# Four seven-product units and one plain unit in the feed-forward stage, in place of three and three

## The chip, the cores and the metric

The kernel runs on one core of a Trainium2 chip. The metric is the device time of one execution in microseconds (us). Five engines take part: PE (TensorE, matmuls; PEld is its weight load), DVE (VectorE), ACT (ScalarE), POOL (GpSimd) and SP (SyncE, which here only issues DMAs). Each engine works through its own instructions in a fixed order and waits for the others by semaphores.

## The reference

One decoder layer in float32 on x of 256 positions by 1024 columns. The first half (block-sparse and differential attention, gates, output projection) is not touched by the change. The second half is

```
x = x + RMSNorm_post(SwiGLU(RMSNorm_pre(x)))
SwiGLU(h) = (silu(h @ w_gate) * (h @ w_up)) @ w_down
# w_gate, w_up: 1024 x 2816    w_down: 2816 x 1024
```

The result has to be accurate to float32. The kernel writes a float32 number as a high part (rounded to PE's fp32r) and a low part (the remainder) and takes three matmuls for one product: high x high, low x high, high x low.

## The kernel before, in words

**f's and units.** The 2816 columns of gate and up are 22 blocks f of 128. The first four are done in another form; the list UNITS (line 54) gives the others: R at f = 4, W at 6, R at 10, W at 12, R at 16, W at 18. The 256 positions are two blocks t = 0 and t = 1 of 128.

**A plain unit (R, line 1140 on)** computes gate and up of two f's: 4 weight pieces, 48 matmuls of 512 columns.

**A seven-product unit (W, line 1090 on)** computes gate and up of four f's, for both t, as a 2 x 2 block product with seven products in place of eight, called 11, T1, T2, 22, T3, 21 and T4. Each has two weight pieces (a and b, 128 x 1024 "pages") and 12 matmuls of 512 columns. The pages of T1 and T3 are sums of two weights: POOL issues DMAs that add the second onto the first (L176). T2 = 11 + T3 and T4 = T2 + 21 are added on DVE (L282), two pages each; in the last unit T4 is made by accumulating DMAs (L288). The products are combined by DVE operations of 128 x 512: u0, u1, the add and the multiply of g0 (around a Silu on ACT) and the multiply of g1 (behind another Silu). The result for t = 0 is called s (or s2), that for t = 1 is called g (or g1).

**Splits.** Each weight piece is split by ACT (copy to the high part, L195) and DVE (subtract for the low part, L198). High and low parts lie in a ring of WB = 5 pairs: the split of a piece can only begin when PE has finished with the piece five places before it. Pages that were loaded lie in 12 buffers, which SP refills (L173) when DVE and ACT have let go of them.

**Down projection.** For each f, PE transposes s and g, ACT takes the high part of the transposed block and DVE the low part (the tile fT), and a weight piece of w_down (wraw) is split; 12 matmuls of 512 columns, called z here, add the result into banks acc. The transposes of a unit's four f's come in the unit behind it, in two sets: first t = 0 (s), then t = 1 (g), both into the same bank, which exists once. So the second set waits until ACT and DVE have read the first. The first set stands behind product 11 and the second behind T1. For t = 1, the second half of the columns goes into two banks of 256 columns each (acc and pv).

**Order.** The order of PE is the list of slots; plan_W gives the places of the products and of z in a unit: 11, T1, T2, z, 22, z, T3, 21, z, T4 in the middle. The order of ACT, DVE and POOL is written out while the slots are walked: granules_ahead (line 404) lets the splits run four pieces ahead of PE, and the operations of a unit that follow a product are put behind the slot that ends it.

**End.** The last four f's of w_down (18 to 21) are split early into memory of their own (wextra) at places given by TAIL_AT, and are used when all else is done: first t = 0, then t = 1, whose second half is done in two pieces of 256, so that the norm of the first piece (ACT L923, DVE L927) can run beside the matmuls of the second.

Of the kernel before, what the change touches and what calls it, by code (L numbers as in the profile page):

```python
# [35 lines left out]
NFF = DFF // P  # L36
# [14 lines left out]
RB = 7  # L51
NWARM = 13
NAT = 4
UNITS = [("R", 4), ("W", 6), ("R", 10), ("W", 12), ("R", 16), ("W", 18)]


def _slopes():
# [8 lines left out]
def tile_hybrid_block(  # L66
# [201 lines left out]

    NTAIL = 4

    TAIL_AT = {"T2": (NFF - 4,), "22": (NFF - 3,), "21": (NFF - 2,), "T3": (NFF - 1,)}
    dr = [raw1(w_down, f * P, 1, 0, 1024) for f in range(NFF)]
    for f in range(NFF):
        dr[f]["name"] = ("d", f)
# [65 lines left out]

    for ui, (kind, f0) in enumerate(UNITS):
        if kind == "R":
            rr = [raw_of([(slice(0, 256), rows(w_gate, 2 * kc * P, 2, f0 * P, 256)),
                          (slice(256, 512), rows(w_up, 2 * kc * P, 2, f0 * P, 256))], 2) for kc in range(4)]
            todo = [lambda kc=kc: job_split(("r", f0, kc), rr[kc]) for kc in range(4)]
            if ui == 0:
                uns = [lambda kc=kc: job_split(("un", kc), nr["un", kc]) for kc in range(1, 4)]
                todo = uns[0:1] + s_jobs(0) + uns[1:2] + s_jobs(1) + uns[2:3] + s_jobs(2, 3, 4, 5) + todo[0:2] + \
                    s_jobs(6) + todo[2:3] + s_jobs(7, 8) + todo[3:4]
            ds = [lambda i=i: job_split(("d", i), dr[i]) for i in units_before(ui)]  # L350
            if ui == 0:
                first = raws_of_W(UNITS[1][1])
                add1 = [lambda i=i: job_add(first["T1"][i], first["11"][i], first["12"][i]) for i in range(2)]
                ds[2:3] += add1[0:1]
                ds += add1[1:2]
            todo += ds
        else:
            b, todo = raws_of_W(f0) if ui > 1 else first, []
            for n in ("11", "T1", "T3", "22", "21"):
                for r in b[n]:  # L360
                    touch(r)
            for n in plan_W(ui):
                if n[0] == "z":
                    todo.append(lambda f=n[1]: job_split(("d", f), dr[f]))
                    continue
                for i in range(2):
                    if n == "T1":
                        todo.append(lambda i=i: job_split(("T1", f0, i), b["T1"][i]))
                        todo.append(lambda i=i: job_add(b["T2"][i], b["11"][i], b["T3"][i]))
                    else:  # L370
                        todo.append(lambda n=n, i=i: job_split((n, f0, i), b[n][i]))
                    if n == "11" and ui == 1:
                        todo.append(lambda i=i: job_add(b["T3"][i], b["12"][i], b["22"][i]))
                    if n == "T2" and ui == len(UNITS) - 1:
                        todo.append(lambda i=i: job_more(b["T2"][i]))
                    if i == 1 and ui == len(UNITS) - 1:
                        for f in TAIL_AT.get(n, ()):
                            todo.append(lambda f=f: job_split(("d", f), dr[f]))
                    if n == "21" and ui < len(UNITS) - 1:
                        todo.append(lambda i=i: job_add(b["T4"][i], b["T2"][i], b["21"][i]))  # L380
        for f in todo:
            f()
# [21 lines left out]
    def granules_ahead(slots, n, most, late):  # L404

        def f(i):
            j, seen = i + 1, set()
            while j < len(slots) and j - i <= most:
                seen |= {x for x, _ in slots[j]["need"]} - {x for x, _ in slots[i]["need"]}
                if len(seen) > n - (i >= len(slots) - late):  # L410
                    break
                j += 1
            return j - i - 1
        return f
# [443 lines left out]
    def out_part(z, name, lhs, ks, t, hf, last, pieces=None):  # L858
        for k in ks:
            for c0, c1, bank in pieces or z[t]:  # L860
                if c0 // 512 == hf:
                    mm3(bank[:, 0:c1 - c0], lhs(k, t), [v[:, 0, c0:c1] for v in W((name, k))],
                        start=k == 0, stop=k == last)

    zb = []

    def z_slots(name, k, lhs, last):
        def pe(hf):
            if not zb:
                zb.extend([(0, 512, ps("acc")), (512, 1024, ps("acc"))] for _ in range(NT))  # L870
                if name == "d":
                    zb[1][1:] = [(512, 768, zb[1][1][2]), (768, 1024, ps("pv"))]
            for t in range(NT):
                out_part(zb, name, lhs, [k], t, hf, last)
        return [dict(pe=lambda h=h: pe(h), need=[((name, k), h)]) for h in range(2)]

    def z_tail(name, ks, lhs, t, last):

        if name == "d" and t == 1:
            return [dict(pe=lambda i=i: out_part(zb, name, lhs, ks[2 * i:2 * i + 2], t, 0, last),  # L880
                         need=[((name, k), 0) for k in ks[2 * i:2 * i + 2]]) for i in range(2)] + \
                   [dict(pe=lambda i=i: out_part(zb, name, lhs, ks, t, 1, last, [zb[t][1 + i]]),
                         need=[((name, k), 1) for k in ks]) for i in range(2)]
        return [dict(pe=lambda h=h, i=i: out_part(zb, name, lhs, ks[2 * i:2 * i + 2], t, h, last),
                     need=[((name, k), h) for k in ks[2 * i:2 * i + 2]]) for h in range(2) for i in range(2)]
# [4 lines left out]
    zgs = []  # L890
# [17 lines left out]
    slots = []  # L908
# [184 lines left out]
    def unit_W(ui, f0, ring):  # L1093

        st, made = {}, {}
        banks = dict(zip("acb", ring))

        def bank(n):
            if n not in st:
                st[n] = ps(banks[n])  # L1100
            return st[n]

        def slots_of(n, bk, a, start, post):
            return [dict(pe=lambda kp=kp: block(bank(bk), a, n, f0, kp, start, True), need=[((n, f0, kp), 0)],
                         post=[lambda: active.append(post())] if kp else []) for kp in range(2)]

        def copy(n, tag, bk, **kw):
            def f():
                made[n] = work.tile([P, 512], F32, tag=tag, name=n, **kw)
                nc.scalar.activation(made[n], st[bk], AF.Copy)  # L1110
                yield
            return f

        def u1():
            nc.vector.tensor_tensor(made["v5"], made["v5"], st["a"], op=OP.subtract)
            yield

        def u0():
            u = made["s2"]
            nc.vector.tensor_tensor(u, st["c"], u, op=OP.subtract)  # L1120
            yield

        def g0():
            g = made["s1"]
            nc.vector.tensor_tensor(g, st["b"], g, op=OP.add)
            yield
            nc.scalar.activation(g, g, AF.Silu, scale=rs2[:, 0:1])
            yield
            u = made["s2"]
            nc.vector.tensor_tensor(u, u, g, op=OP.mult)  # L1130

        def g1():
            g = made["g1"] = work.tile([P, 512], F32, tag="e", name="g1", bufs=4)
            nc.scalar.activation(g, st["a"], AF.Silu, scale=rs2[:, 1:2])
            yield
            nc.vector.tensor_tensor(g, g, made["v5"], op=OP.mult)

        how = {"11": ("a", A(0, 0), True, copy("s1", "ph0", "a", bufs=1)),
               "T1": ("c", R_(0), True, copy("v5", "pl0", "c", bufs=1)),
               "T2": ("a", R_(1), False, copy("s2", "e", "a", bufs=4)), "22": ("c", R_(3), False, u0),  # L1140
               "T3": ("a", R_(2), False, u1), "21": ("b", A(0, 1), True, g0), "T4": ("a", A(1, 1), False, g1)}
        sl = [s for n in plan_W(ui) for s in (z_slots("d", n[1], f_of, NFF - 1) if n[0] == "z" else slots_of(n, *how[n]))]
        return sl, [lambda tag: f_T({0: lambda: made["s2"]}, f0, 4, tag), lambda tag: f_T({1: lambda: made["g1"]}, f0, 4, tag)]

# [64 lines left out]


    def norm3(t):
        pn.append(post_norm(zb[t], gp2, eps3[:, t:t + 1], zgs[t]))
        pn[t][0](0)

    def finish(t):
        piece, r, zg = pn[t]
        piece(len(zb[t]) - 1)
        for c0, c1 in ((0, 384), (384, 768), (768, 1024)):
            add_x(zg, zg, r, xt[:, t, :], c0, c1)
            nc.sync.dma_start(out[0, t * P:(t + 1) * P, c0:c1], zg[:, c0:c1])  # L1220
# [33 lines left out]
```

## Time and profile before

| | us |
|---|---|
| median of 3 runs (lowest to highest) | 382.33 (381.61 to 383.94) |
| the profiled execution's own time | 383.71 |
| its span | 381.9 |
| PE busy | 369.8 (97%) |
| DVE busy | 300.2 (79%) |
| ACT busy | 233.9 (61%) |
| POOL busy | 43.8 (11%) |
| mean granted clock of PE | 0.993 |

The span is the time from the first to the last instruction of the profiled execution. Busy times overlap. A start-to-start distance shorter than the duration means that an engine begins the next instruction before the last one's end. In the trace, whi and wlo are the high and low parts in the ring, wpage and wraw the loaded pieces, h2h and h2l the normalized x. The feed-forward units from W6 on lie at 237 to 262 (W6), 262 to 286 (R10), 286 to 311 (W12), 311 to 334.5 (R16) and from 334.5 on (W18).

### The profile page before, as it was taken

The page shows a single profiled execution, that of the slowest core. Times are in us where ns is not written, and L with a number is a line of the kernel's source. Part 1 is how long each engine was busy: PE and PEld are TensorE (multiplying, and loading weights), DVE is VectorE, ACT ScalarE, POOL GpSimd, SP SyncE. Part 2 cuts the span into 40 slices and gives each one's busy share as a digit, 9 for nine tenths or more (in the row PEclk, how much of TensorE's full clock was granted, in tenths as well). Part 3 has the DMA queues.
Part 4 walks back from the last instruction along what each step waited for, and adds up shares of the span by engine and source line. Part 5 has one row for each costly group of instructions (what it writes and reads, how often), then busy time and mean ns, then how long its engine had stood idle before and what let it go on. Part 6 is the DMA issues. An engine that isn't in the chain of part 4 may idle for free.

```text
span 381.9 us, 6158 instructions
## 1 busy us (share of the span) xinstructions
PE 369.8 (97%) x2212; PEld 324.4 (85%) x2212; DVE 300.2 (79%) x542; ACT 233.9 (61%) x431; POOL 43.8 (11%) x61
## 2 busy tenths in 40 slices
PE   6999999999999999999999999999999999999893
PEld 4799989999999999898888888888888888888683
DVE  3799787899978757798669969998578885799534
ACT  3985576768665865574469453866548655487221
POOL 0099600000001000000000000220002200020000
PEclk9999999999999999999999999999999999999898
DMA  6988746253654553587216998899959997151003
GB/s 191 389 288 306 207 128 206 66 167 111 218 156 127 184 198 128 187 250 230 92 57 204 399 391 277 207 329 289 379 166 191 342 298 217 57 83 27 3 0 110
DMA packets 41665, 74.98 MB, mean 196 GB/s; under 512 B 3218, under 2 KB 15523, under 8 KB 41635
## 3 DMA queue, kind: packets, MB, share of 16 engines
q1 hardware_dynamic: 38914, 69.36, 54.3%
q0 software_dynamic: 2720, 5.24, 8.0%
q8 instruction: 17, 0.28, 0.3%
q14 instruction: 14, 0.11, 0.1%
HBM read 73.54 MB, written 1.05 MB: 195 GB/s over the span
## 4 chain that ended last, share of the span: by engine, by line
PE 88%; DVE 5%; DMA 2%; issue 2%; ACT 2%; SPq 1%; POOLq 0%; DVEq 0%; ACTq 0%
PE acc L227 14%; PE acc L228 13%; PE acc L229 13%; PE acc L663 5%; PE sb L227 4%; PE sb L228 4%; PE sb L229 4%; PE sa L228 4%; PE sa L227 4%; PE sa L229 4%; PE t L227 3%; PE t L228 3%; PE t L229 3%; DVE wlo L198 3%; PE pv L228 2%; PE pv L229 2%
## 5 line engine op out<-in xcount | busy, mean ns | idle before, releaser
L198 DVE TENSOR_TENSOR wlo<-wraw,whi 128x512 fp32r<-128x512 f32 (+1 forms) x137 | 116.7, 873 | 35.7 <-ACT whi L195 35.3
L195 ACT ACTIVATE whi<-wraw 128x512 fp32r<-128x512 f32 (+1 forms) x136 | 99.2, 765 | 31.0 <-PE acc L228 14.5
L227 PE MATMUL acc<-hTh,whi 128*128 128x256 f32 x256 | 73.1, 286 | 0.5 <-DVE q L602 0.5
L229 PE MATMUL acc<-hTh,wlo 128*128 128x256 f32 x256 | 71.8, 281 | 0.0
L228 PE MATMUL acc<-hTl,whi 128*128 128x256 f32 x256 | 71.8, 281 | 0.0
L198 DVE TENSOR_TENSOR wlo<-wpage,whi 128x1024 fp32r<-128x1024 f32 x42 | 50.8, 1220 | 8.4 <-ACT whi L195 8.2
L195 ACT ACTIVATE whi<-wpage 128x1024 fp32r<-128x1024 f32 x42 | 43.9, 1060 | 18.7 <-PE pv L229 8.4
L227 PEld LDWEIGHTS acc<-hTh,whi 128*128 128x128 f32 x256 | 48.3, 189 | 0.8 <-DVE q L602 0.7
L228 PEld LDWEIGHTS acc<-hTl,whi 128*128 128x128 f32 x256 | 48.3, 189 | 0.0
L229 PEld LDWEIGHTS acc<-hTh,wlo 128*128 128x128 f32 x256 | 48.2, 188 | 0.0
L227 PE MATMUL acc<-whi,fT 128*128 128x512 f32 x72 | 26.5, 368 | 0.0
L229 PE MATMUL acc<-whi,fT 128*128 128x512 f32 x72 | 26.2, 365 | 0.0
L228 PE MATMUL acc<-wlo,fT 128*128 128x512 f32 x72 | 26.2, 364 | 0.0
L176 POOL DMA_DIRECT2D wpage<-in_w_up_dram x8 | 9.8, 1225 | 89.6 <-DMA wpage<-in_w_gate_dram 70.5
L708 ACT ACTIVATE e<-e,nmx 128x256 f32<-128x256 f32 (+1 forms) x32 | 14.3, 447 | 5.7 <-DVE nmx L705 5.4
L282 DVE TENSOR_TENSOR wpage<-wpage 128x1024 f32<-128x1024 f32 x14 | 17.0, 1217 | 0.0
L228 PEld LDWEIGHTS acc<-wlo,fT 128*128 128x128 f32 x72 | 13.5, 188 | 2.6
L227 PEld LDWEIGHTS acc<-whi,fT 128*128 128x128 f32 x72 | 13.5, 188 | 2.5
L229 PEld LDWEIGHTS acc<-whi,fT 128*128 128x128 f32 x72 | 13.5, 188 | 2.3
L227 PE MATMUL t<-whi,h2h 128*128 128x512 f32 x36 | 15.1, 420 | 0.0
L228 PE MATMUL t<-wlo,h2h 128*128 128x512 f32 x36 | 15.0, 416 | 0.0
L229 PE MATMUL t<-whi,h2l 128*128 128x512 f32 x36 | 14.7, 409 | 0.0
(347 smaller groups left out, 858.6 us busy)
## 6 DMA issues: line engine op xcount, KB each, us to landing
wraw<-in_w_in_dram SPq DMA_DIRECT2D x37, 512.0 KB, 4.7
wraw<-in_w_down_dram SPq DMA_DIRECT2D x22, 512.0 KB, 8.9
wpage<-in_w_gate_dram SPq DMA_DIRECT2D x16, 512.0 KB, 10.1
wpage<-in_w_up_dram SPq DMA_DIRECT2D x12, 512.0 KB, 8.4
wraw<-in_w_out_dram SPq DMA_DIRECT2D x8, 512.0 KB, 3.3
wpage<-in_w_up_dram POOLq DMA_DIRECT2D x8, 512.0 KB, 8.9
wraw<-in_w_gate_dram SPq DMA_DIRECT2D x12, 256.0 KB, 6.2
wraw<-in_w_up_dram SPq DMA_DIRECT2D x12, 256.0 KB, 6.8
```

What stands on the lines that cost most here:

```text
L176: nc.gpsimd.dma_start(q["tile"], q["more"][n], accum_op=OP.add)
L195: nc.scalar.activation(hi, src, AF.Copy)
L198: nc.vector.tensor_tensor(lo, src, hi.bitcast(F32), op=OP.subtract)
L227: nc.tensor.matmul(dst, lh, rh, start=start, stop=False, **kw)
L228: nc.tensor.matmul(dst, lh, rl, start=False, stop=False, **kw)
L229: nc.tensor.matmul(dst, ll, rh, start=False, stop=stop, **kw)
L282: nc.vector.tensor_tensor(dst["flat"], a["flat"], b["flat"], op=OP.add)
L663: nc.tensor.matmul(acc[t], l[:, k, ts_], r, start=k == 0 and n == 0, stop=k == KT - 1 and n == 2)
L708: nc.scalar.activation(e[:, m, 0:n], e[:, m, 0:n], AF.Exp, bias=nmx[:, m:m + 1], scale=-1.0, accum_out=sm[:, m:m + 1])
```

## The change

UNITS becomes R at 4, then W at 6, 10, 14 and 18: the plain units at 10 and 16 and the W at 12 give way to two W units at 10 and 14. So three times a W stands directly behind a W. The early splits of the last four down pieces move from behind T2, 22, 21 and T3 of the last unit to before its first product, behind T1, 22 and T4. They are no longer counted by granules_ahead. The second half of t = 1 in the down projection is one bank of 512 columns; only in the last four f's it is addressed as two halves of 256, of the same bank. In the last unit the multiply of g0 follows its Silu without a slot between them.

```diff
--- before.py
+++ after.py
@@ -51,7 +51,7 @@
 RB = 7
 NWARM = 13
 NAT = 4
-UNITS = [("R", 4), ("W", 6), ("R", 10), ("W", 12), ("R", 16), ("W", 18)]
+UNITS = [("R", 4), ("W", 6), ("W", 10), ("W", 14), ("W", 18)]
 
 
 def _slopes():
@@ -268,7 +268,7 @@
 
     NTAIL = 4
 
-    TAIL_AT = {"T2": (NFF - 4,), "22": (NFF - 3,), "21": (NFF - 2,), "T3": (NFF - 1,)}
+    TAIL_AT = {"": (NFF - 4,), "T1": (NFF - 3,), "22": (NFF - 2,), "T4": (NFF - 1,)}
     dr = [raw1(w_down, f * P, 1, 0, 1024) for f in range(NFF)]
     for f in range(NFF):
         dr[f]["name"] = ("d", f)
@@ -356,6 +356,13 @@
             todo += ds
         else:
             b, todo = raws_of_W(f0) if ui > 1 else first, []
+
+            def spare(n):
+                if ui == len(UNITS) - 1:
+                    for f in TAIL_AT.get(n, ()):
+                        todo.append(lambda f=f: job_split(("d", f), dr[f]))
+
+            spare("")
             for n in ("11", "T1", "T3", "22", "21"):
                 for r in b[n]:
                     touch(r)
@@ -373,9 +380,8 @@
                         todo.append(lambda i=i: job_add(b["T3"][i], b["12"][i], b["22"][i]))
                     if n == "T2" and ui == len(UNITS) - 1:
                         todo.append(lambda i=i: job_more(b["T2"][i]))
-                    if i == 1 and ui == len(UNITS) - 1:
-                        for f in TAIL_AT.get(n, ()):
-                            todo.append(lambda f=f: job_split(("d", f), dr[f]))
+                    if i == 1:
+                        spare(n)
                     if n == "21" and ui < len(UNITS) - 1:
                         todo.append(lambda i=i: job_add(b["T4"][i], b["T2"][i], b["21"][i]))
         for f in todo:
@@ -406,7 +412,7 @@
         def f(i):
             j, seen = i + 1, set()
             while j < len(slots) and j - i <= most:
-                seen |= {x for x, _ in slots[j]["need"]} - {x for x, _ in slots[i]["need"]}
+                seen |= {x for x, _ in slots[j]["need"] if x not in place} - {x for x, _ in slots[i]["need"]}
                 if len(seen) > n - (i >= len(slots) - late):
                     break
                 j += 1
@@ -860,7 +866,7 @@
             for c0, c1, bank in pieces or z[t]:
                 if c0 // 512 == hf:
                     mm3(bank[:, 0:c1 - c0], lhs(k, t), [v[:, 0, c0:c1] for v in W((name, k))],
-                        start=k == 0, stop=k == last)
+                        start=k == 0, stop=k == last, skip_group_check=pieces is not None and c0 == 768)
 
     zb = []
 
@@ -868,18 +874,20 @@
         def pe(hf):
             if not zb:
                 zb.extend([(0, 512, ps("acc")), (512, 1024, ps("acc"))] for _ in range(NT))
-                if name == "d":
-                    zb[1][1:] = [(512, 768, zb[1][1][2]), (768, 1024, ps("pv"))]
             for t in range(NT):
                 out_part(zb, name, lhs, [k], t, hf, last)
         return [dict(pe=lambda h=h: pe(h), need=[((name, k), h)]) for h in range(2)]
 
+    def halves(z):
+
+        return [z[0], (512, 768, z[1][2][:, 0:256]), (768, 1024, z[1][2][:, 256:512])]
+
     def z_tail(name, ks, lhs, t, last):
 
         if name == "d" and t == 1:
             return [dict(pe=lambda i=i: out_part(zb, name, lhs, ks[2 * i:2 * i + 2], t, 0, last),
                          need=[((name, k), 0) for k in ks[2 * i:2 * i + 2]]) for i in range(2)] + \
-                   [dict(pe=lambda i=i: out_part(zb, name, lhs, ks, t, 1, last, [zb[t][1 + i]]),
+                   [dict(pe=lambda i=i: out_part(zb, name, lhs, ks, t, 1, last, [halves(zb[t])[1 + i]]),
                          need=[((name, k), 1) for k in ks]) for i in range(2)]
         return [dict(pe=lambda h=h, i=i: out_part(zb, name, lhs, ks[2 * i:2 * i + 2], t, h, last),
                      need=[((name, k), h) for k in ks[2 * i:2 * i + 2]]) for h in range(2) for i in range(2)]
@@ -1125,7 +1133,8 @@
             nc.vector.tensor_tensor(g, st["b"], g, op=OP.add)
             yield
             nc.scalar.activation(g, g, AF.Silu, scale=rs2[:, 0:1])
-            yield
+            if ui < len(UNITS) - 1:
+                yield
             u = made["s2"]
             nc.vector.tensor_tensor(u, u, g, op=OP.mult)
 
@@ -1209,12 +1218,12 @@
 
 
     def norm3(t):
-        pn.append(post_norm(zb[t], gp2, eps3[:, t:t + 1], zgs[t]))
+        pn.append(post_norm(halves(zb[t]) if t else zb[t], gp2, eps3[:, t:t + 1], zgs[t]))
         pn[t][0](0)
 
     def finish(t):
         piece, r, zg = pn[t]
-        piece(len(zb[t]) - 1)
+        piece(1 + t)
         for c0, c1 in ((0, 384), (384, 768), (768, 1024)):
             add_x(zg, zg, r, xt[:, t, :], c0, c1)
             nc.sync.dma_start(out[0, t * P:(t + 1) * P, c0:c1], zg[:, c0:c1])
```

Three places in the order of the instructions follow. The first is DVE at the end of W6 and the beginning of the unit behind it. Before, that unit is R10: from g0's add (L1125) over the multiplies of g0 (L1130) and g1 (L1136) to the low part of the transposed s (the first L1050).

```order
L198 TENSOR_TENSOR wlo<-wpage,whi 128x1024
L198 TENSOR_TENSOR wlo<-wraw,whi 128x1024
L1125 TENSOR_TENSOR s_3104<-sa,s_3104 128x512
L198 TENSOR_TENSOR wlo<-wraw,whi 128x1024
L1130 TENSOR_TENSOR s_3159<-s_3159,s_3104 128x512
L198 TENSOR_TENSOR wlo<-wraw,whi 128x1024
L1136 TENSOR_TENSOR g_3295<-g_3295,v_3131 128x512
L198 TENSOR_TENSOR wlo<-wraw,whi 128x1024
L1050 TENSOR_TENSOR fT<-sb,fT 128x512
L198 TENSOR_TENSOR wlo<-wraw,whi 128x1024 x2
```

In the changed kernel the unit behind W6 is W10; the same operations are L1133, L1139, L1145 and the first L1058.

```order
L1133 TENSOR_TENSOR s_3087<-sa,s_3087 128x512
L198 TENSOR_TENSOR wlo<-wpage,whi 128x1024
L1139 TENSOR_TENSOR s_3142<-s_3142,s_3087 128x512
L198 TENSOR_TENSOR wlo<-wpage,whi 128x1024
L282 TENSOR_TENSOR wpage<-wpage 128x1024
L198 TENSOR_TENSOR wlo<-wpage,whi 128x1024
L282 TENSOR_TENSOR wpage<-wpage 128x1024
L198 TENSOR_TENSOR wlo<-wpage,whi 128x1024
L1145 TENSOR_TENSOR g_3283<-g_3283,v_3114 128x512
L198 TENSOR_TENSOR wlo<-wpage,whi 128x1024
L198 TENSOR_TENSOR wlo<-wraw,whi 128x1024
L1058 TENSOR_TENSOR fT<-sb,fT 128x512
```

Between g0's add and the low part of s there were three splits (of R10's pieces); now there are six (11b, T1a, T1b, T2a, T2b and one of the down projection) and two adds of pages.

The second place is DVE at the beginning of the last unit, W18, in the changed kernel, from the split of W14's last page but one on; the rows with wextra are early splits of down pieces, L1133 and L1139 are g0 of W14.

```order
L198 TENSOR_TENSOR wlo<-wpage,whi 128x1024
L198 TENSOR_TENSOR wextra<-wraw,wextra 128x1024
L198 TENSOR_TENSOR wlo<-wpage,whi 128x1024
L1133 TENSOR_TENSOR s_3583<-t,s_3583 128x512
L198 TENSOR_TENSOR wlo<-wpage,whi 128x1024
L1139 TENSOR_TENSOR s_3656<-s_3656,s_3583 128x512
L198 TENSOR_TENSOR wlo<-wpage,whi 128x1024
L282 TENSOR_TENSOR wpage<-wpage 128x1024
L198 TENSOR_TENSOR wlo<-wpage,whi 128x1024
L282 TENSOR_TENSOR wpage<-wpage 128x1024
L198 TENSOR_TENSOR wextra<-wraw,wextra 128x1024
L198 TENSOR_TENSOR wlo<-wpage,whi 128x1024
```

Two early splits stand among the first pages of W18, one ahead of 11a and one behind the second T2 add (L282). Behind these rows follow the split of T2a, the multiply of g1, the split of T2b and one split of the down projection, and then the low part of s; so both early splits lie before it.

The third place is PE near its end: the last matmuls of t = 1's first half of 256 columns and the first of its second half. Before:

```order
L229 MATMUL acc<-wextra,fT 128x256
L227 MATMUL acc<-wextra,fT 128x256
L228 MATMUL acc<-wextra,fT 128x256
L229 MATMUL acc<-wextra,fT 128x256
L227 MATMUL pv<-wextra,fT 128x256
L228 MATMUL pv<-wextra,fT 128x256
```

And in the changed kernel:

```order
L229 MATMUL acc<-wextra,fT 128x256
L227 MATMUL acc<-wextra,fT 128x256
L228 MATMUL acc<-wextra,fT 128x256
L229 MATMUL acc<-wextra,fT 128x256
L227 MATMUL acc<-wextra,fT 128x256 [waits DVE_49]
L228 MATMUL acc<-wextra,fT 128x256
```

The second half has the bank of the first, and its first matmul waits for DVE; before, it had the bank pv and no wait.

## Rows read from the trace of the kernel before

**Rows 1.** Page, part 1: busy time, share of span, instructions of each engine
```profile
PE 369.8 (97%) x2212; PEld 324.4 (85%) x2212; DVE 300.2 (79%) x542; ACT 233.9 (61%) x431; POOL 43.8 (11%) x61
```

**Rows 2.** Windows: busy (count) of PE, PEld, DVE, ACT, POOL; clock, DMA, GB/s
```profile
262.00:285.80 23.80, 23.80 (x122) 19.93 (x121) 17.86 (x20) 13.05 (x17) 0.00 (x0) 1.00 0.87 268
285.80:310.90 25.10, 25.10 (x115) 20.53 (x115) 20.49 (x20) 16.64 (x18) 4.81 (x4) 1.00 1.02 275
```

**Rows 3.** PE's waits, 200 to 382 us: engine, line, releaser, total, times, longest
```profile
PE sb L1043 <- DVE s L1130: 1.7, 1, 1.7
```

**Rows 4.** Timeline of PE, 256 to 270 us: start, duration, instruction
```profile
258.54 0.28 PE L227 MATMUL acc<-whi,fT 128*128 128x256 f32 x1
...
259.23 0.40 PE L227 MATMUL sb<-whi,h2h 128*128 128x512 f32 x1
...
262.03 0.39 PE L227 MATMUL t<-whi,h2h 128*128 128x512 f32 x1
...
264.83 0.60 PE L1043 MATMUL sb<-ident,s 128*128 128x128 f32 x4
...
268.07 0.60 PE L1043 MATMUL sb<-ident,g 128*128 128x128 f32 x4
```

**Rows 5.** Timeline of all engines, 353 to 365 us
```profile
356.72 1.23 DVE L198 TENSOR_TENSOR wlo<-wpage,whi 128x1024 fp32r<-128x1024 f32 x1 [1.74 <-ACT whi L195]
357.86 0.69 DVE L1130 TENSOR_TENSOR s<-s,s 128x512 f32<-128x512 f32 x1
...
358.60 0.66 PE L1043 MATMUL sb<-ident,s 128*128 128x128 f32 x4 [1.73 <-DVE s L1130]
...
359.29 0.62 PE L227 MATMUL t<-whi,h2h 128*128 128x512 f32 x1
...
363.71 0.39 PE L227 MATMUL acc<-wextra,fT 128*128 128x512 f32 x1
```

**Rows 6.** Windows behind the wait: columns as in the second group
```profile
358.60:362.86 4.26, 4.23 (x13) 3.26 (x14) 1.23 (x2) 0.60 (x1) 0.00 (x0) 0.60 0.00 0
362.86:366.66 3.80, 3.80 (x19) 3.04 (x18) 0.69 (x1) 0.69 (x1) 0.00 (x0) 1.00 0.00 0
```

**Rows 7.** Timeline of all engines, 372 to 376 us
```profile
373.93 0.28 PE L227 MATMUL pv<-wextra,fT 128*128 128x256 f32 x1
...
374.19 0.38 ACT L923 ACTIVATE scr<-acc 128x256 bf16<-128x256 f32 x1 [0.74 <-PE acc L229]
...
374.70 0.42 DVE L927 TENSOR_TENSOR zg<-acc,gp 128x256 f32<-128x256 f32 x1 [0.53 <-ACT scr L923]
```

**Rows 8.** Timeline of DVE, 252 to 260 us
```profile
253.38 1.21 DVE L282 TENSOR_TENSOR wpage<-wpage 128x1024 f32<-128x1024 f32 x1
254.52 1.22 DVE L198 TENSOR_TENSOR wlo<-wraw,whi 128x1024 fp32r<-128x1024 f32 x1
...
256.79 0.68 DVE L1115 TENSOR_TENSOR v<-v,sb 128x512 f32<-128x512 f32 x1
257.38 1.22 DVE L198 TENSOR_TENSOR wlo<-wpage,whi 128x1024 fp32r<-128x1024 f32 x1
```

**Rows 9.** Timeline of ACT, 254 to 257 us
```profile
254.71 1.06 ACT L195 ACTIVATE whi<-wpage 128x1024 fp32r<-128x1024 f32 x1 [1.13 <-DVE wpage L282]
255.68 1.04 ACT L195 ACTIVATE whi<-wraw 128x1024 fp32r<-128x1024 f32 x1
```

**Rows 10.** Timeline of POOL, 240 to 345 us: its accumulating DMAs
```profile
254.57 2.53 POOL L176 DMA_DIRECT2D wpage<-in_w_up_dram  x2 [9.49 <-DMA wpage<-in_w_up_dram]
...
299.38 2.50 POOL L176 DMA_DIRECT2D wpage<-in_w_up_dram  x2 [8.19 <-DVE wlo L198]
```

**Rows 11.** Line 176's issues in 254 to 257 us: their way to landing
```profile
DMA to landing us min/median/max: 9.7/11.1/12.4
```

**Rows 12.** Line 176's issues in 299 to 302 us: their way to landing
```profile
DMA to landing us min/median/max: 8.2/9.5/10.9
```

## The prediction

> **What bounds the kernel now.** The page comes first: PE is busy for nearly all of the span [rows 1], so a change is worth what it takes out of PE's stream or puts into it as idle time. The windows, one a unit, show the feed-forward stage: in a plain unit (262.00 to 285.80) and the seven-product unit W12 behind it (285.80 to 310.90) PE is busy throughout, and DVE for 75% and 82% [rows 2]: it has room, but not much. PE's list of waits is the third view: from 200 us on it waits once, near the end [rows 3]. Before, then, each split arrives in time. Whether it still does is settled on DVE, whose order is fixed: a late item delays all behind it.
>
> **What PE loses.** Two plain units (96 matmuls of 512 columns) give way to one of seven products (84). Twelve go; T4's twelve of them take 259.23 to 262.03, 2.80 us [rows 4]: **-2.8**. The down pages' six matmuls of 256 columns become three of 512; six take 258.54 to 259.23 [rows 4], 0.69, and three of 512 a quarter of 2.80, 0.70: **0**. These are 54 of the 66 matmuls that disappear, and they bring nothing.
>
> **The last unit's g0 multiply.** The one wait of PE, 1.73, is for this multiply, which stood behind a page split that itself began late, after 1.74 for its copy [rows 5]. Without the pause behind the Silu it goes ahead of that split: **-1.7**. [...] Without the wait: **-1.6**.
>
> **The last twelve matmuls.** The two 256-column halves of t=1 now share a bank, so the second waits until ACT and DVE have read the first. Before, it began at 373.93 in a bank of its own, while ACT (374.19) and DVE (374.70 plus 0.42) read the first half [rows 7]. Now it can begin at 375.12: **+1.2**. Below this it is worth nothing if the two read out sooner; above it, about 1.5 with a hand-over.
>
> **A seven-product unit behind another.** This is the large term. A unit's PE time is 84 matmuls and 4 down pages of 12, 132 x 0.233 = 30.8, and two sets of transposes at 0.36 [rows 4]: 31.5 us. DVE has 18 splits and 4 adds of 1024 columns, from start to start 1.135 (253.38 to 254.52, and 254.52 to 256.79 with one not shown), and 7 operations of 512 at 0.60 (256.79 to 257.38) [rows 8]: 25.0 + 4.2 = 29.2 us, 93% of PE's. That fits on average; the phase does not. The previous unit's f's are transposed in two sets into one bank, so the second (of g1) waits until DVE has taken the low part of the first. Without a wait it comes 6.04 us behind the unit's first product (262.03 to 268.07 [rows 4]). Before, a plain unit's few splits stood ahead of that low part. Now there are page splits and adds, as the listing of DVE's order shows.
> - W6 to W10: the T4 split begins at 257.38 [rows 8]; 11a, g0's add, 11b and the multiply follow, so T1a starts at about 262.0. From T1a to the low part are seven items of 1.135 and two of 0.60, 9.15: it ends at about 271.2, and at 271.7 with 0.5 of hand-overs (an estimate: the last item lasts 0.69, not 0.60, PE followed DVE by 0.05 in [rows 5], and two of the items wait for a Silu). Against 268.07: **+3.6**.
> - W10 to W14: the ring of five holds DVE back. 21a can be split only when PE has left 22a; from there to the unit's end is 22b, z, T3, 21, z and T4, 1.4 + 5 x 2.8 = 15.4 us. A copy on ACT of 0.97 from start to start [rows 9] and the hand-overs take 1.5. Then seven items of 1.135 and two of 0.60 follow, 9.15, before 11a, which starts 4.75 before the end. From 11a to the low part are nine of 1.135 and four of 0.60, 12.6; with 0.5 the low part is there 8.35 into the unit against 6.04: **+2.3**. It is 1.0 if 11a starts as early as the ring admits it (6.0 before the end), 3.5 if as late as in W6 (258.52, 3.5 before 262.03). I take 2.3, since ring and order together give it.
> - W14 to W18: a tail split stands ahead of 11a and another behind the T2 adds; both lie ahead of the low part, 2 x 1.135: **+4.6**.
>
> Sum of the three 10.5. z's first matmuls take the set that is done by then, so the second low part costs nothing.
>
> **T3's pages.** The second T2 add of W10 needs T3b. Its accumulating DMAs are issued at 254.57 and 255.84 [rows 10] and land 9.7 and 12.4 us later, at 264.3 and 268.3 [rows 11]. Nothing ahead of them changes. By DVE's own time that add would start at 265.4; now at 268.3: **+2.9**. The lower end is 0, if the queue is lighter. At the next transitions the pages come early enough: W12's pair was issued 13.6 us into its unit (299.38 against 285.8) [rows 10], and the second lands 10.9 behind its own issue [rows 12], some 25.8 into a unit of 31.5. Behind the added accumulates POOL has no other work here; SP issues fewer transfers (no plain half pages).
>
> **The clock.** The single idle time of 1.73 was followed by a stretch at 0.60 [rows 5, 6]. The first and third stall are longer than that: 1.6 each. The second is of about that size: I take half, 0.8. **+4.0**, with 0 and 4.9 as ends.
>
> **Duration or distance.** DVE's 1024-column items last 1.21 to 1.22 but start 1.135 apart; those of 512 last 0.68 and start 0.59 apart [rows 8]. At the durations the three transitions would cost 9 x 1.22 + 4 x 0.68 - 12.6 = 1.1 more at the second, 0.8 and 1.3 at the others, 3.2 in all. I keep the distances, since nothing in the rows holds the next item back. [...]
>
> **Sum.** -2.8 - 1.7 - 1.6 + 1.2 + 10.5 + 2.9 + 4.0 = +12.5. On the profiled execution's own 383.71 that is 396.2; it lies 1.4 above the median, so against 382.33 the forecast is **395**. Within 1% means 378.5 to 386.2, about what a measurement here can tell.
>
> **Rivals.**
> - *The stalls come, but smaller* (0.26): T3 is in time, or the clock stays. Without the clock term 391; without T3's wait 392; without both 388. For: the clock was seen to fall only once here. Against: the idle time before it was shorter than the ones expected.
> - *Faster: DVE keeps its lead* (0.08). The place is the low part of the first transposes. If it is there 6.04 us into each unit, no stall and no clock term arise, and 382.3 - 2.8 - 3.3 + 1.2 = 377.4. For: DVE's share of 93% leaves 2.3 us a unit. Against: 11a would have to start 12.6 + 0.5 - 6.04 = 7.1 before the end of the unit, and the ring admits it at 6.0. The point from which it decides is 7.1; W6 shows 3.5 [rows 8].
> - *Within 1%* (0.10): stalls of 1.0 at the ring's limit give 382.3 - 4.9 + 3.0 = 380.4; the shorter W6 stall of 3.6 with the others near 1.0 to 2.3 and full clock gives 383 to 385.
> - *The pages are late everywhere* (0.06): now every unit has four accumulating transfers. If T3 lands 3 us late at the second and third transition too, 395 + 6 = 401. Against: 25.8 of 31.5 above.
> - *DVE's items follow at their durations* (0.02), once it has no waits to overlap: 395 + 3.2 = 398. The rows show back-to-back items already at the shorter distance [rows 8]. [...]
>
> The forecast itself has 0.48. The predicted time is its 395. The range 387 to 400 holds it, the smaller stalls and the items at their durations; outside are the faster case, most of the case within 1% and the late pages. Faster by over 1%: 0.08; within 1%: 0.10; slower: 0.82.
>
> **What would show it.** In the changed kernel's profile: PE's waits list three new rows, at the second transposes of W10, W14 and W18, ended by DVE (the low part), of some 6.5, 2.3 and 4.6 us; the clock in the stretches behind them lies under 1.00; DVE's items in W10's first 12 us stand without gaps, apart from one before the second T2 add, which ends when T3b lands. In the last unit the wait of 1.73 is absent. At the end one gap of about 1.2 lies on PE between the two halves. The forecast is wrong if the transposes' waits are absent, or if DVE's 11a starts over 7 us before a unit's end.

## Result: slower by 3.6%, and the waits where they were forecast

The changed kernel takes 396.61 us (median of 4 executions, 394.83 to 397.23) against 382.74 (4 executions): a ratio of 1.036, interval 1.033 to 1.039. The profiled execution's own time is 396.04, its span 394.2, 12.3 longer than before.

Part 1 of the page after the change (against [rows 1]): PE's busy time has hardly moved, though it has 66 matmuls fewer; its share fell from 97% to 94%.

```profile
PE 371.1 (94%) x2146; PEld 322.2 (82%) x2146; DVE 313.9 (80%) x553; ACT 242.3 (61%) x438; POOL 48.5 (12%) x65
```

PE's waits from 200 us to the end (line, tile, what ended the wait, us in total, times, longest), against the single one in [rows 3]:

```profile
PE sb L1051 <- DVE fT L1058: 6.4, 1, 6.4
PE sa L1051 <- DVE fT L1058: 4.3, 1, 4.3
PE t L1051 <- DVE fT L1058: 2.2, 1, 2.2
PE acc L227 <- DVE zg L935: 1.1, 1, 1.1
PE sa L228 <- DVE wlo L198: 0.3, 1, 0.3
```

The first three are the second transposes of W10, W18 and W14, each waiting for the low part of the first set (L1058); the fourth is the gap between the two halves of one bank. Together they are 14.0 us. The wait for g0's multiply is gone. The next rows, PE's timeline, show the three waits and the product behind each (280.30 and 352.16 are the first matmuls of z); the second transposes of R10 in [rows 4], their counterpart before, had no wait.

```profile
274.78 1.11 PE L1051 MATMUL sb<-ident,g 128*128 128x128 f32 x4 [6.42 <-DVE fT L1058]
275.55 0.78 PE L227 MATMUL t<-whi,S 128*128 128x512 f32 x1
...
280.30 0.40 PE L227 MATMUL acc<-whi,fT 128*128 128x512 f32 x1
...
310.86 0.66 PE L1051 MATMUL t<-ident,g 128*128 128x128 f32 x4 [2.16 <-DVE fT L1058]
311.27 0.48 PE L227 MATMUL sa<-whi,S 128*128 128x512 f32 x1
...
346.81 1.12 PE L1051 MATMUL sa<-ident,g 128*128 128x128 f32 x4 [4.25 <-DVE fT L1058]
347.58 0.78 PE L227 MATMUL sb<-whi,S 128*128 128x512 f32 x1
...
352.16 0.39 PE L227 MATMUL acc<-whi,fT 128*128 128x512 f32 x1
```

DVE's timeline in W10, from the split of T1a to the low part (its distances can be set beside [rows 8]):

```profile
261.65 1.23 DVE L198 TENSOR_TENSOR wlo<-wpage,whi 128x1024 fp32r<-128x1024 f32 x1
264.53 1.23 DVE L282 TENSOR_TENSOR wpage<-wpage 128x1024 f32<-128x1024 f32 x1 [1.65 <-DMA wpage<-in_w_up_dram]
265.67 1.22 DVE L198 TENSOR_TENSOR wlo<-wpage,whi 128x1024 fp32r<-128x1024 f32 x1
268.55 1.23 DVE L282 TENSOR_TENSOR wpage<-wpage 128x1024 f32<-128x1024 f32 x1 [1.66 <-DMA wpage<-in_w_up_dram]
269.69 1.22 DVE L198 TENSOR_TENSOR wlo<-wpage,whi 128x1024 fp32r<-128x1024 f32 x1
270.83 0.69 DVE L1145 TENSOR_TENSOR g<-g,v 128x512 f32<-128x512 f32 x1
271.43 1.22 DVE L198 TENSOR_TENSOR wlo<-wpage,whi 128x1024 fp32r<-128x1024 f32 x1
272.90 1.22 DVE L198 TENSOR_TENSOR wlo<-wraw,whi 128x1024 fp32r<-128x1024 f32 x1 [0.25 <-ACT whi L195]
274.04 0.68 DVE L1058 TENSOR_TENSOR fT<-sb,fT 128x512 fp32r<-128x512 f32 x1
```

Items that follow each other start 1.14 and 0.60 apart, as before; the two gaps, 1.65 and 1.66, end with a DMA that adds onto T3's page. Those DMAs landed as in [rows 11]:

```profile
DMA to landing us min/median/max: 9.8/11.2/12.5
```

The windows behind the three waits (PE, PEld, DVE, ACT and POOL busy, then the granted clock; columns as in [rows 6]):

```profile
274.78:280.50 5.72, 5.72 (x17) 4.71 (x18) 3.77 (x4) 2.61 (x4) 0.00 (x0) 0.57 1.03 224
310.86:314.20 3.34, 3.34 (x17) 2.80 (x18) 2.14 (x2) 2.52 (x3) 0.00 (x0) 1.00 0.94 196
346.81:352.20 5.39, 5.39 (x17) 4.46 (x18) 2.90 (x3) 1.55 (x2) 0.00 (x0) 0.58 0.92 164
```

Behind the first and the third wait the granted clock was 0.57 and 0.58 on average: 0.50 up to 279.7 and 351.4, and 1.00 from there on (a stretch at 0.50 is called "half clock" below). Behind the second it stayed at 1.00.

### The profile page after: what moved, and what is told of

The parts are those of the page before. It is cut to its first block, busy times and chain, and to the rows that moved or that the text cites. A ratio compares the mean times of both kernels' runs of the same rounds, so it can differ in the third digit from the quotient of the medians.

```text
span 394.2 us, 6056 instructions
## 1 busy us (share of the span) xinstructions
PE 371.1 (94%) x2146; PEld 322.2 (82%) x2146; DVE 313.9 (80%) x553; ACT 242.3 (61%) x438; POOL 48.5 (12%) x65
## 5 line engine op out<-in xcount | busy, mean ns | idle before, releaser
L198 DVE TENSOR_TENSOR wlo<-wraw,whi 128x512 fp32r<-128x512 f32 (+1 forms) x129 | 107.0, 852 | 27.2 <-ACT whi L195 26.8
L195 ACT ACTIVATE whi<-wraw 128x512 fp32r<-128x512 f32 (+1 forms) x128 | 90.8, 748 | 34.1 <-PE acc L228 14.5
L198 DVE TENSOR_TENSOR wlo<-wpage,whi 128x1024 fp32r<-128x1024 f32 x56 | 68.1, 1221 | 13.5 <-ACT whi L195 13.3
L195 ACT ACTIVATE whi<-wpage 128x1024 fp32r<-128x1024 f32 x56 | 58.5, 1059 | 30.0 <-DVE wpage L282 9.6
L229 PE MATMUL acc<-whi,fT 128*128 128x512 f32 x72 | 28.3, 393 | 0.0
L227 PE MATMUL acc<-whi,fT 128*128 128x512 f32 x72 | 28.3, 393 | 0.0
L176 POOL DMA_DIRECT2D wpage<-in_w_up_dram x12 | 14.6, 1218 | 107.2 <-DMA wpage<-in_w_gate_dram 57.7
L282 DVE TENSOR_TENSOR wpage<-wpage 128x1024 f32<-128x1024 f32 x18 | 21.9, 1219 | 3.3 <-DMA wpage<-in_w_up_dram 3.3
L489 POOL TENSOR_TENSOR rs_r<-rs_e,mhalf 128x2 f32<-128x2 f32 x4 | 3.2, 794 | 93.6 <-DVE rs_e L486 93.6
L931 ACT ACTIVATE scr<-acc 128x512 bf16<-128x512 f32 (+1 forms) x9 | 5.0, 552 | 14.5 <-PE acc L229 14.5
L934 POOL TENSOR_TENSOR rs_r<-rs_e,mhalf 128x1 f32<-128x1 f32 x4 | 2.2, 553 | 91.3 <-DVE rs_e L933 91.3
```

The costliest lines, as they stand in the source:

```text
L176: nc.gpsimd.dma_start(q["tile"], q["more"][n], accum_op=OP.add)
L195: nc.scalar.activation(hi, src, AF.Copy)
L198: nc.vector.tensor_tensor(lo, src, hi.bitcast(F32), op=OP.subtract)
L227: nc.tensor.matmul(dst, lh, rh, start=start, stop=False, **kw)
L229: nc.tensor.matmul(dst, ll, rh, start=False, stop=stop, **kw)
L282: nc.vector.tensor_tensor(dst["flat"], a["flat"], b["flat"], op=OP.add)
```

## Experiments

The theory: the second transposes wait because the low part of the first set stands late in DVE's order, behind pages that a plain unit did not have; T3's late pages make W10's wait longer; the early splits make W18's longer. The main rival: three seven-product units on end are simply too much for DVE (93% of PE's time) and the page transfers, and the wait at the transposes is only where this shows. The time of the kernel before, run beside each group of runs, was 382.1 to 382.8.

**1. The second transposes in a bank of their own.**

```diff
-sl = sl[0:2] + [left[0](ring[2])] + sl[2:4] + [left[1](ring[2])] + sl[4:]
+sl = sl[0:2] + [left[0](ring[2])] + sl[2:4] + [left[1]("pv" if kind == "W" and i > 1 else ring[2])] + sl[4:]
```

> The changed kernel, with the second transposes (g1) of W10, W14 and W18 in the bank pv, so that they need not wait until DVE has read the first set. Theory (the second set waits for the low part of the first, which stands late in DVE's order): what is left is the wait for g1's multiply, which DVE ends 3.2, 3.2 and 2.9 us earlier than the low part. The three waits go from 6.4, 2.2, 4.3 to about 3.2, 0, 1.4 us, 8.3 us less; 396.6 becomes 388 with the clock as it was, 384 to 386 if the slow stretches behind them go too. Rival (DVE and the pages are too slow for three seven-product units in a row, whatever the bank): the time comes back as waits of PE at the splits behind, and the total stays at 395 to 397.

Measured 387.94 (387.31 to 388.53). PE's waits:

```profile
PE pv L1051 <- DVE g L1145: 4.7, 2, 3.3
PE acc L229 <- DVE fT L1058: 2.0, 3, 1.1
PE acc L227 <- DVE zg L935: 1.1, 1, 1.1
```

What is left at the transposes is the multiply of g1, 3.3 at W10, 1.5 at W18, none at W14, as expected. New is 2.0 at z: its third matmul takes the low part, which is no earlier than before. That the time still came out at the expected 388 is in part luck: only W10's wait is followed by half clock here, which gives back some 3 us (an estimate from the stretches behind the waits, 4.6 lost before and 1.4 now), and the 2.0 at z took most of it. The rival's 395 is ruled out.

**2. The old places of the early splits.**

```diff
-TAIL_AT = {"": (NFF - 4,), "T1": (NFF - 3,), "22": (NFF - 2,), "T4": (NFF - 1,)}
+TAIL_AT = {"T2": (NFF - 4,), "22": (NFF - 3,), "21": (NFF - 2,), "T3": (NFF - 1,)}
```

> The changed kernel with the early splits of the last four down pieces behind T2, 22, 21 and T3 of the last unit, as before. Theory: two splits of 1.135 us go from in front of the low part in W18, so only its wait shrinks, from 4.3 to 2.0 us; 396.6 becomes 394.3, or 392.2 if the clock behind it stays at 1.00 as it did behind W14's 2.2 us. Rival (the splits' place does not matter, only their number): the wait stays at 4.3 and the time at 396 to 397.

Measured 395.66 (393.37 to 397.31), no clear difference. W18's wait went from 4.3 to 3.3, not to 2.0. The expectation misread the edit: behind T2 the first early split still stands in front of the low part, so one split moved out, not two, and one split is 1.135. Run 8 moves both.

**3. T3's pages without the second load in W10** (half of that sum is left out).

```diff
-"T3": two((w_up, 0), (w_up, 4)),
+"T3": two((w_up, 0)) if f == 10 else two((w_up, 0), (w_up, 4)),
```

> The changed kernel; in W10 T3's pages are loaded without the second weight being added (part of the sum is left out), so no accumulating DMA is waited for. Theory: DVE's two waits of 1.65 and 1.66 us at the T2 adds of W10 go, W10's low part is ready 3.3 us earlier, PE's wait there goes from 6.4 to 3.1 us; 396.6 becomes 393.3 (391 if the clock stays up). The other two waits stay at 2.2 and 4.3. Rival (the pages are not what is late; DVE would do the same work later anyway): 6 us of wait remain and 396 to 397.

Measured 392.65 (391.64 to 393.96). The waits of W10, W14 and W18 are 3.5, 2.1 and 4.2; only W10's moved, by 2.9. The pages' part of the loss is real. It is W10's alone: in the changed kernel's list of waits of DVE, from 250 us on, T3's pages stand with just the two waits of W10.

```profile
DVE wpage L282 <- DMA wpage<-in_w_up_dram: 3.3, 2, 1.7
```

**4. The kernel before with half a bank each at the end.** The core of its edit, as in the change:

```diff
-                zb[1][1:] = [(512, 768, zb[1][1][2]), (768, 1024, ps("pv"))]
+        return [z[0], (512, 768, z[1][2][:, 0:256]), (768, 1024, z[1][2][:, 256:512])]
```

> The kernel before, with only the change of banks: the second half of t=1 in the down projection is one bank of 512 columns, in two halves of 256 of the same bank at the end; 54 fewer matmuls. Theory: the matmuls bring nothing, and PE waits 1.1 us at the end between the two halves: 383.8 against 382.7. Rival (fewer, larger matmuls save issue time): 2 to 4 us faster, 379 to 381, less the 1.1.

Measured 383.23 (382.38 to 384.85), ratio 1.0026 (1.0005 to 1.0047). PE's new wait for DVE's read of the first half is 1.1; the 54 matmuls fewer bring nothing that shows. The rival's 2 to 4 us are ruled out.

**5. Bank of its own, and T1's and T3's pages loaded first.**

```diff
-for n in ("11", "T1", "T3", "22", "21"):
+for n in ("T1", "T3", "11", "22", "21") if ui > 1 else ("11", "T1", "T3", "22", "21"):
```

> As the run with the second transposes in pv, and T1's and T3's pages are loaded ahead of 11's from W10 on, so that T3's accumulating DMAs are issued some ten us earlier. Theory: the two waits of DVE (1.7 each) at W10's T2 adds go, g1's multiply is ready 3.4 us earlier, and PE's wait of 3.3 at W10 shrinks to under 0.5; 387.9 becomes 384, or 383 if the slow clock behind it goes too. Rival (the queue as a whole is late, not T3's place in it): 11's pages land late instead, PE waits at the head of W10 or at the splits, and the time stays at 387 to 389.

Measured 384.10 (383.70 to 384.36). PE's waits:

```profile
PE acc L229 <- DVE fT L1058: 3.2, 3, 1.5
PE pv L1051 <- DVE g L1145: 1.7, 2, 1.5
PE acc L227 <- DVE zg L935: 1.1, 1, 1.1
```

At W10 the wait for g1's multiply is 0.27; what remains of that line is W18's 1.5. The pages are not late as a whole; T3 stood too far back in the queue. z's waits for the low part grew from 2.0 to 3.2.

**6. The kernel before without the pause ahead of g0's multiply.**

```diff
             nc.scalar.activation(g, g, AF.Silu, scale=rs2[:, 0:1])
-            yield
+            if ui < len(UNITS) - 1:
+                yield
```

> The kernel before, with only the pause between the last unit's g0 Silu and its multiply taken out. Theory: PE's one wait (1.7 us) goes, and with it the stretch of half clock that follows it in some executions (about 1.5 us between the upper and the lower of the times seen): 380.3 against 382.3, and no execution above 381.5. Rival (T4's second page split, now behind the multiply, is late instead): a wait of 0.5 to 1.2 at T4, 381.5 to 382.5.

Measured 381.33 (380.84 to 382.84), ratio 0.998 (0.9963 to 0.9998): less than half of what the theory gave. The one wait of PE moved:

```profile
PE t L227 <- DVE v L1115: 1.4, 1, 1.4
```

The multiply is on time, but u1 (L1115), which frees T4's bank, now stands behind T4's second page split, and PE waits 1.4 for it. These rows of DVE and PE show it (multiply, split, u1, T4's first matmul):

```profile
355.20 0.69 DVE L1131 TENSOR_TENSOR s<-s,s 128x512 f32<-128x512 f32 x1 [0.79 <-ACT s L1127]
356.16 1.22 DVE L198 TENSOR_TENSOR wlo<-wpage,whi 128x1024 fp32r<-128x1024 f32 x1 [0.26 <-ACT whi L195]
357.30 0.68 DVE L1115 TENSOR_TENSOR v<-v,t 128x512 f32<-128x512 f32 x1
...
358.13 0.47 PE L227 MATMUL t<-whi,h2h 128*128 128x512 f32 x1 [1.38 <-DVE v L1115]
```

That is near the rival. Two of the ten executions were still 1.5 longer.

**7. Five edits together:** the bank of run 1, the load order of run 5, early splits behind 22, 21, T3 and T4, t = 1's last half in one piece, and the low part in DVE's order right behind the copy of the high part:

```diff
             nc.scalar.activation(h, b, AF.Copy)
-            yield
+            if f0 < 6:
+                yield
             nc.vector.tensor_tensor(l, b, h.bitcast(F32), op=OP.subtract)
+            if f0 >= 6:
+                yield
```

> The changed kernel with five edits: second transposes in pv; T1 and T3 loaded ahead of 11; no early split ahead of the low parts in W18; the low part of fT put into DVE's order right behind its high part's copy; t=1's last half in one piece of 512 columns. Theory (the units themselves cost less PE time; all that was lost is order): PE's waits between 250 us and the end add up to under 2 us; the time is 382.3 - 2.8 (matmuls) - 1.7 (the multiply) + up to 2 = 378 to 380. Rival (DVE at 93% of PE's time in three units on end cannot keep up): waits of 3 to 6 us stay, 382 to 386.

Measured 377.99 (377.65 to 378.51), 0.989 of the kernel before (0.986 to 0.991): faster than both. PE's waits, all that is left, and the page's first part:

```profile
PE sb L227 <- DVE v L1126: 0.4, 1, 0.4
PE pv L1051 <- DVE g L1148: 0.3, 1, 0.3
```

```profile
PE 366.1 (97%) x2134; PEld 318.1 (85%) x2134; DVE 312.2 (83%) x552; ACT 241.6 (64%) x436; POOL 48.6 (13%) x65
```

DVE's timeline in W10 of this kernel, the rows from the second T2 add on:

```profile
265.08 1.22 DVE L282 TENSOR_TENSOR wpage<-wpage 128x1024 f32<-128x1024 f32 x1
...
267.35 0.68 DVE L1148 TENSOR_TENSOR g<-g,v 128x512 f32<-128x512 f32 x1
...
269.09 0.68 DVE L1059 TENSOR_TENSOR fT<-sb,fT 128x512 fp32r<-128x512 f32 x1
...
271.95 0.68 DVE L1059 TENSOR_TENSOR fT<-pv,fT 128x512 fp32r<-128x512 f32 x1
```

The multiply ends at 268.03 instead of 271.52, and the low part (L1059) at 269.77 instead of 274.72. DVE does the same 22 page and piece operations a unit; three seven-product units on end do fit. The rival's 382 to 386 is ruled out.

**8. Both early splits behind the low part, nothing else.**

```diff
-TAIL_AT = {"": (NFF - 4,), "T1": (NFF - 3,), "22": (NFF - 2,), "T4": (NFF - 1,)}
+TAIL_AT = {"22": (NFF - 4,), "21": (NFF - 3,), "T3": (NFF - 2,), "T4": (NFF - 1,)}
```

> The changed kernel with the early splits behind 22, 21, T3 and T4 of the last unit, so that none stands in front of the low part (in the run with the old places one still did). Theory: W18's wait goes from 4.3 to 2.0 us; the waits of W10 and W14 stay at 6.4 and 2.2; 396.6 becomes 394.3, or 392.5 where the clock stays up behind it. Rival: a late down piece at the end, PE waits there for wextra, no gain.

Measured 394.07 (391.57 to 395.28). The waits are 6.4, 2.1 and 2.1: W18's shrank by 2.2, two splits, and the others stayed.

**9. Run 7 with the transposes in one bank.**

```diff
-sl = sl[0:2] + [left[0](ring[2])] + sl[2:4] + [left[1]("pv" if kind == "W" and i > 1 else ring[2])] + sl[4:]
+sl = sl[0:2] + [left[0](ring[2])] + sl[2:4] + [left[1](ring[2])] + sl[4:]
```

> As the run with all five edits, but the second transposes again in the bank of the first. Theory (it is DVE's order that made the bank a wait, and the bank costs only what the low part is late): the low part of the first set was ready 1.7 us after the second set's turn in W10 and 0.8 after it in W14 and W18, so waits of about 1.7, 0.8, 0.8 or a little less come back; 378.0 becomes 380.5 to 381.3. Rival (the bank itself is the cause, the order matters little): waits of 3 to 6 us each, over 386.

Measured 381.44 (380.69 to 382.26). Waits of 2.0, 0.7 and 0.7 at the transposes:

```profile
PE sb L1051 <- DVE fT L1059: 2.0, 1, 2.0
PE sa L1051 <- DVE fT L1059: 0.7, 1, 0.7
PE t L1051 <- DVE fT L1059: 0.7, 1, 0.7
```

That is 3.4 us of wait from the shared bank, once low part, pages and early splits are mended; the time is just above the expected 380.5 to 381.3. The theory holds and the rival is ruled out. But bank and order don't split the 12.9 of the changed kernel into two fixed shares: with its own bank and the old order 6.7 were left (run 1, 4.7 at the transposes and 2.0 at z), with the new order and the old bank 3.4, and with both 0.7 (run 7).

**10. Run 7 with two pieces at the end.**

```diff
-        if False:
+        if name == "d" and t == 1:
...
-        pn.append(post_norm(zb[t], gp2, eps3[:, t:t + 1], zgs[t]))
+        pn.append(post_norm(halves(zb[t]) if t else zb[t], gp2, eps3[:, t:t + 1], zgs[t]))
...
-        piece(1)
+        piece(1 + t)
...
+    t1[2]["post"] = [lambda: pn[1][0](1)]
```

> As the run with all five edits, but t=1's last half again in two pieces of 256 columns of one bank. Theory: PE's wait of 1.1 us between the pieces comes back, and the last reads by ACT and DVE are 0.5 shorter: 0.6 slower, 378.6. Rival (the shorter end pays for the wait): 378.0 or less.

Measured 379.32 (378.89 to 380.96) against 377.99: 1.3 more, or 0.9 by the ratios to the kernel before that ran beside each (0.9909 and 0.9886), with PE's wait of 1.1 back. Expected was 0.6, and the measurement doesn't tell the two apart. That the pieces pay for their wait is not what the times show: the fastest execution here (378.89) is above the slowest of run 7 (378.51). The intervals of the two ratios overlap, though, so the size stays open.

**11. Run 7 with the low part late.**

```diff
-            if f0 < 6:
-                yield
+            yield
             nc.vector.tensor_tensor(l, b, h.bitcast(F32), op=OP.subtract)
-            if f0 >= 6:
-                yield
```

> As the run with all five edits, but fT's low part again behind a split of the down projection in DVE's order. Theory: with the bank of its own the low part is waited for only by the third matmul of z; it is one to two splits of 1.135 later, so waits of 0.6 to 1.5 a unit come back at z, 2 to 3 us in all: 380 to 381. Rival (z has other matmuls ahead that cover it): 378.

Measured 381.53 (381.03 to 383.05). z waits for the low part for 2.7 in three places, the longest 1.5; the low part's place alone is worth 3.1 by the ratios (0.9968 and 0.9886). The rival's 378 is ruled out.

The load order and the early splits were not taken out of run 7 one by one; what they are worth is known only from runs 5 and 8, beside other waits.

## Why the prediction was right

The forecast was 395 in a range of 387 to 400, with 0.82 for slower. By its own steps, with the profiled execution's 12.3 beside the sum of 12.5:

| step | predicted | measured |
|---|---|---|
| twelve matmuls fewer | -2.8 | -2.8 (worked out, not isolated) |
| 54 matmuls of 256 columns fewer | 0 | nothing that shows (run 4) |
| the multiply's wait | -1.7 | -1.7, and a new 0.3 for a split in W10; alone -0.8, as a wait of 1.4 came up at T4 (run 6) |
| half clock behind it | -1.6 | -2.0 in this trace; not in the medians |
| halves of one bank | +1.2 | +1.1; run 4: +0.9 in time |
| W6 to W10, with T3's pages | +3.6 and +2.9 | 6.4; run 3: 3.5 and 2.9 |
| W10 to W14 | +2.3 | 2.2 |
| W14 to W18 | +4.6 | 4.3; run 8: 2.2 of it the two splits |
| half clock behind the waits | 1.6 + 0.8 + 1.6 | 2.4, 0, 2.2 |

The measured entries, with 12.9 for the three waits, sum to -2.8 - 1.7 + 0.3 - 2.0 + 1.1 + 6.4 + 2.2 + 4.3 + 4.6 = +12.4, against 12.3.

**The transitions** were worked out from DVE's distances, the ring of five and the order, and each came within 0.3. In W10, DVE's row of L1058 starts at 274.04; T1a's start at 261.65 plus 8.55 of items, 3.3 of waits for pages and 0.25 for a copy gives 273.8. In W14 the ring shows as it was worked out: ACT's copy of 21a waits for PE's matmuls of 22a (sa), DVE's split of it follows at 288.50, and 11a's is the second of the two splits from 296.51.

```profile
287.40 1.06 ACT L195 ACTIVATE whi<-wpage 128x1024 fp32r<-128x1024 f32 x1 [0.34 <-PE sa L229]
288.50 1.23 DVE L198 TENSOR_TENSOR wlo<-wpage,whi 128x1024 fp32r<-128x1024 f32 x1 [0.18 <-ACT whi L195]
296.51 2.35 DVE L198 TENSOR_TENSOR wlo<-wpage,whi 128x1024 fp32r<-128x1024 f32 x2
302.52 0.39 PE L227 MATMUL sa<-whi,h2h 128*128 128x512 f32 x1
```

The last row is W14's first product. So 11a's split starts at about 297.65, 4.9 before it, where 4.75 was taken, and PE goes on with the second transposes 8.3 behind it (310.86), where 8.35 was.

**T3's pages.** The prediction let only the second T2 add wait. Both did, 1.65 and 1.66, because T3a landed at 264.4 and DVE's turn for the first add was at 262.9. By the prediction's own numbers (T1a's split at 262.0, T3a at 264.3) it would have been late too. That left the sum as it is, since T3b's landing sets the second add either way: 3.3, near the 2.9 taken.

**The clock** came near in sum (4.6 against 4.0) but not in its parts, which is in part luck. The prediction's 1.6 for one stretch is what T4's twelve matmuls took longer in the kernel before, 359.29 to 363.71 [rows 5], 4.42 in place of 2.80. The measured loss is counted here from the transposes on, against the 0.36 + 2.80 of a stretch without a wait: 274.78 to 280.30 is 5.52, so 2.4; 346.81 to 352.16 gives 2.2, and the second wait nothing to speak of. For the wait in the kernel before, 358.60 to 363.71 [rows 5] is 5.11, so 2.0. Not all of this is the clock: in run 4 the same stretch, behind the same wait, took 3.57 at a granted clock of 1.00.

The -1.6 does not belong in a sum on the median. The kernel before was executed 23 times beside runs 5 to 8: 15 times it took 381.3 to 382.3 (mean granted clock 0.994 to 0.998) and 8 times 383.0 to 383.8 (0.992 to 0.994). The profiled execution of before (383.71) is one with the drop; by these groups the median of 382.33 is one without. So the prediction took the drop off twice, as -1.6 in the sum and again as the 1.4 between 383.71 and 382.33. Without the -1.6 the sum is 14.1, and 382.33 + 14.1 is 396.4, against 396.61 measured.

**Distances, not durations.** A 1024-column item lasted 1.22 in the rows of W10, and back to back the items again start 1.14 apart; the case in which they follow at their durations did not come.

**The rivals.** DVE did not keep its lead: the low part came 2 to 6 us late in each of the three units. That three such units do not fit at all was not among the rivals; run 7 shows that they do. Late pages of T3 at the second and third transition did not come either: DVE's list of waits (under run 3) has none there.

## What to carry to other kernels

Compare engines not only by their share of a stage but by where, in the fixed order of the second-busiest one, the item stands that the busiest one waits for next: here DVE had some 2.3 us to spare in each unit by the prediction's estimate, and PE still lost 2 to 6 near its start. Where one buffer is written twice in a stage, the last reader of the first content sets the time of the second (here DVE's low part, with waits of 6.4, 2.2 and 4.3); a second buffer or a reader moved forward in its order are each worth a try before the larger work split is given up. A term that occurs in only some executions, as a drop of the clock, belongs in the sum with its share, not whole.

## What the runs showed of the clock

PE's granted clock did not follow the length of an idle time alone. Eight waits of 3.25 us and more in the traces of the changed kernel and of runs 1, 2, 3 and 8 were all followed by a stretch at half clock (0.50; matmuls of 512 columns start 0.43 apart in it, at 1.00 0.23), which made the next twelve matmuls last 3.8 to 5.3 us in place of 2.8. Of eleven waits of 1.4 to 2.2 us at the transposes or, in run 6, behind them, four were followed by one: 1.73 in the kernel before, 2.1 in runs 2 and 8, 2.0 in run 9; not 2.16 in the changed kernel, 2.1 in runs 3 and 8, 1.7 in run 4, 1.5 in runs 1 and 5, and 1.4 in run 6. The same wait of W14 (2.1 to 2.2) was followed by half clock in run 2 (0.52 from 311.36 to 314.90),

```profile
311.36 1.03 PE L1051 MATMUL t<-ident,g 128*128 128x128 f32 x4 [2.14 <-DVE fT L1058]
312.04 0.78 PE L227 MATMUL sa<-whi,S 128*128 128x512 f32 x1
312.61 0.63 PE L228 MATMUL sa<-wlo,S 128*128 128x512 f32 x1
```

where the matmuls start 0.43 to 0.57 apart, and by full clock in the changed kernel (the window from 310.86 above, 1.00). What tells them apart these runs don't show.
